# Rotary embedding on one core: tables of 16 rows, batches as runs of 2048 rows, the first tile stored whole

## The chip, the cores and the metric

The kernel runs on one core of a Trainium2 chip. The metric is the device time of one execution in microseconds (us); lower is better. Each time below is from the profile of one execution or from repeated runs without a profile. The engines named are PE (TensorE, matrix products), DVE (VectorE), ACT (ScalarE), POOL (GpSimd) and SP (SyncE). Transfers between DRAM and the on-chip memory (SBUF) are issued by ACT and SP and carried by 16 DMA engines, which take packets from two queues: q10 holds what ACT issues (loads), q1 what SP issues (stores).

## What is computed

A rotary position embedding in fp32 on x of shape (16, 512, 1024): 16 batches, 512 positions, 16 heads of 64. The output has the shape (16, 512, 16, 64).

```python
x = x.reshape(batch, seq, num_heads, head_dim)
x1, x2 = (x[..., :half_dim].copy(), x[..., half_dim:].copy())
cos = cos[None, :, None, :].copy()
sin = sin[None, :, None, :].copy()
rotated = np.concatenate([x1 * cos - x2 * sin, x1 * sin + x2 * cos], axis=-1)
```

33.5 MB are read and 33.5 MB written. cos and sin are 512 x 32 each; a row of x (one position of one batch) uses the table row of its position.

## The kernel before

**Layout.** The 16 x 512 = 8192 rows of x are cut into 8 runs of two batches, 1024 consecutive rows each. Partition p of a run holds 8 consecutive rows (R2), 32 KB, so that one run is one piece of 4 MB, contiguous in DRAM. A run is one tile of 8 rows per partition, except for the first and the last run, which are two tiles of 4 rows (R1) each: tiles 0 and 1, then 2 to 7, then 8 and 9. Below, "row u" is the u-th of the 64 rows per partition, in order; one row is 128 partitions x 1024 elements. Because the 64 partitions of a batch hold 8 positions each, the table on a partition needs 8 rows.

**Tables.** cos and sin are loaded in the natural order, 4 positions to a partition, into `stage` (L173). The table in the layout of x comes from PE: `pick` (L176, made by ACT from an identity matrix) selects every second partition, once from 0 and once from 1, and two products of `pick` with `stage` (L199, L200) put 2 x 4 table rows into `tab_ps`, in PSUM. ACT then copies the sines to SBUF twice, negated (L178) and as they are (L179), as `s_sb`. DVE reads the cosines directly from `tab_ps`. POOL and DVE start with x only when `s_sb` is there (L244, L262). For the row that DVE multiplies by the sine itself (row 3 of a whole tile, V2), one DVE instruction writes the negated sine row beside the plain one (`v_table`, L265).

**Per row.** DVE multiplies x by cos into one of 3 PSUM buffers `t1_ps` (L286). POOL multiplies x, with its halves swapped, by the signed sine into one of 8 buffers `t2_sb` (L252), mostly two rows at a time; for V2 rows DVE does it (L279). The sum is made in one of two ways and overwrites x in `x_sb`: DVE adds both (L297), or, for rows u with u % 8 in 1, 3, 5 (PE2), PE adds `t2` to the PSUM buffer through the identity (L216) and ACT copies the result (L183).

**Order and queues.** Each engine's program is written out by hand, with semaphores between them; nothing is scheduled by a compiler. `x_sb` is a ring of 40 rows, five 4 MB tiles. ACT issues the loads of tiles 0 to 5 at once (L152), with the loads of cos and sin behind tile 0. The other four are issued in ACT's program after row 17, 25 and 33 (LAG): before each, ACT waits until the store of the rows that stood in that place has landed (L186; `sem_out`, `stores_of`), and ACT's copies (L183) of later rows stand behind this wait. SP issues a store for each tile when its last row is added (L160): so the first run leaves as two stores of 2 MB, after row 3 and after row 7. At the end SP waits for all stores that nobody else has waited for (L161).

Of the kernel before, what the change touches and what calls it, by code (L numbers as in the profile page):

```python
# [6 lines left out]
def bass_split_heads_rope_kernel(  # L7
# [16 lines left out]
    batch, seq, dim = x.shape  # L24
    H = int(num_heads)
    HD = dim // H
    HALF = HD // 2
    P = 128
    R1 = seq // P
    R2 = 2 * R1  # L30
    assert R1 * P == seq and R1 == 4 and batch % 2 == 0

    fp32 = mybir.dt.float32
    bf16 = mybir.dt.bfloat16
# [2 lines left out]
    COPY = mybir.ActivationFunctionType.Copy  # L37


    runs = batch // 2  # L40
    tiles = []
    for c in range(runs):
        if c in (0, runs - 1):
            tiles += [(c, 0, R1), (c, R1, R1)]
        else:
            tiles.append((c, 0, R2))
    NT = len(tiles)
    RING = 5 * R2

# [2 lines left out]
    EARLY = (NU - RING) // R2  # L52


    V_ROW = 3
    PE2 = [R1 <= u < NU - R1 and u % R2 in (1, 3, 5) for u in range(NU)]
    V2 = [tiles[t][2] == R2 and r == V_ROW for t, r in rows]

    def count(flags):
        return [sum(flags[: u + 1]) for u in range(NU)]  # L60
# [16 lines left out]
    with ExitStack() as stack:  # L77
        x_sb = stack.enter_context(nc.sbuf_tensor([P, RING, H, 2, HALF], fp32))
        t2_sb = stack.enter_context(nc.sbuf_tensor([P, NT2, H, 2, HALF], fp32))
        stage = stack.enter_context(nc.sbuf_tensor([P, 2, R1 * HALF], fp32))  # L80
        s_sb = stack.enter_context(nc.sbuf_tensor([P, R2, 2, HALF], fp32))
        ident = stack.enter_context(nc.sbuf_tensor([P, P], fp32))
        pick = stack.enter_context(nc.sbuf_tensor([P, 2, 2, P // 2], fp32))
        zero = stack.enter_context(nc.sbuf_tensor([P, BANK], bf16))
        tab_ps = stack.enter_context(nc.psum_tensor([P, 2, 2, R1, HALF], fp32))
        t1_ps = stack.enter_context(nc.psum_tensor([P, NT1, H * HD], fp32))
        sem_in = [stack.enter_context(nc.semaphore(f"in{t}")) for t in range(NT)]
        sem_out = [stack.enter_context(nc.semaphore(f"out{k}")) for k in range(EARLY)]
# [14 lines left out]
        sem_a = stack.enter_context(nc.semaphore("act"))  # L103

        def table_row(u):
            return u % R2

        xr = x.rearrange("(c b) (s r) d -> c (b s) r d", b=2, r=R2)
        outr = out.rearrange("(c b) (s r) h d -> c (b s) r (h d)", b=2, r=R2)
        xs = x_sb[:].rearrange("p n h t d -> p n (h t d)")  # L110

        def in_dram(view, t):
            c, r0, n = tiles[t]
            return view[c][:, r0:r0 + n, :].rearrange("p r d -> p (r d)")

        def in_sbuf(t):
            c, r0, n = tiles[t]
            k = (c * R2 + r0) % RING
            return x_sb[:, k:k + n].rearrange("p n h t d -> p (n h t d)")

        def where(u):
# [3 lines left out]
        def swapped(k):  # L125
            return x_sb[:, k, :, ::-1, :]
# [19 lines left out]

        def stores_of(k):

            return sum(c == k for c, _, _ in tiles)

        def load(eng, t):
            eng.dma_start(in_sbuf(t), in_dram(xr, t)).then_inc(sem_in[t], 16)  # L152
# [1 line left out]
        def on_sync(sp):  # L154
            for u in range(NU):
                t, r, k = where(u)
                if r == tiles[t][2] - 1:
                    wait_added(sp, u)
                    k = u // R2
                    sp.dma_start(in_dram(outr, t), in_sbuf(t)).then_inc(sem_out[k] if k < EARLY else sem_rest, 16)  # L160
            sp.wait_ge(sem_rest, 16 * sum(stores_of(k) for k in range(EARLY, NU // R2)))  # L161

        def on_scalar(ae):
            later = {}
            for t, (c, r0, n) in enumerate(tiles):
                if c * R2 + r0 + n <= RING:
                    load(ae, t)
                else:

                    later.setdefault((c * R2 + r0 - RING) // R2 * R2 + R2 - 1 + LAG, []).append(t)  # L170
                if t == 0:
                    for i, (table, sem) in enumerate(((cos, sem_cos), (sin, sem_sin))):
                        ae.dma_start(stage[:, i, :], table.rearrange("(s r) d -> s (r d)", r=R1)).then_inc(sem, 16)  # L173

            ae.wait_ge(sem_i, 2)
            ae.activation(pick[:], ident[:].rearrange("q (s h) -> q h s", h=2)[:, :, None, :].broadcast_to([P, 2, 2, P // 2]), COPY).then_inc(sem_g, 1)  # L176
            ae.wait_ge(sem_t, 2)
            ae.activation(s_sb[:, :, 0, :].rearrange("p (h r) d -> p h r d", h=2), tab_ps[:, :, 1], COPY, scale=-1.0)  # L178
            ae.activation(s_sb[:, :, 1, :].rearrange("p (h r) d -> p h r d", h=2), tab_ps[:, :, 1], COPY).then_inc(sem_s, 1)  # L179
            for u in range(NU):  # L180
                if PE2[u]:
                    ae.wait_ge(sem_e, n_pe[u])
                    ae.activation(xs[:, u % RING, :], t1_ps[:, u % NT1, :], COPY).then_inc(sem_a, 1)  # L183
                for t in later.get(u, ()):
                    k = tiles[t][0] - RING // R2
                    ae.wait_ge(sem_out[k], 16 * stores_of(k))  # L186
                    load(ae, t)

        def on_tensor(pe):
            pe.wait_ge(sem_z, 1)  # L190
            for k in range(NT1):
                for b in range(EH):
                    pe.matmul(  # L193
                        t1_ps[:, k, b * BANK:(b + 1) * BANK], zero[:, 0:P], zero[:], start=True, stop=True
                    ).then_inc(sem_w, 1)
            pe.wait_ge(sem_g, 1)
            pe.wait_ge(sem_cos, 16)
            pe.wait_ge(sem_sin, 16)
            for h in range(2):  # L199
                pe.matmul(  # L200
                    tab_ps[:, h].rearrange("p c r d -> p (c r d)"),
                    pick[:, h].rearrange("q b s -> q (b s)"),
                    stage[:].rearrange("q c f -> q (c f)"),
                    start=True,
                    stop=True,
                ).then_inc(sem_t, 1)
            for u in range(NU):
                if not PE2[u]:
                    continue
                pe.wait_ge(sem_m, u + 1)  # L210

                if not V2[u]:
                    pe.wait_ge(sem_p, n_pool[u])
                t2 = t2_sb[:, u % NT2, :, :, :].rearrange("p h t d -> p (h t d)")
                for b in range(EH):
                    ins = pe.matmul(  # L216
                        t1_ps[:, u % NT1, b * BANK:(b + 1) * BANK],
                        ident[:],
                        t2[:, b * BANK:(b + 1) * BANK],
                        start=False,  # L220
                        stop=True,
                        skip_group_check=True,
                    )
                ins.then_inc(sem_e, 1)
# [34 lines left out]
        def on_vector(ve):  # L259
            ve.memset(zero[:], 0.0).then_inc(sem_z, 1)  # L260
            ve.wait_ge(sem_w, NT1 * EH)
            ve.wait_ge(sem_s, 1)  # L262

            def v_table():
                ve.tensor_scalar_mul(tab_ps[:, 0, 1, V_ROW - 1, :], tab_ps[:, 0, 1, V_ROW, :], -1.0).then_inc(sem_c, 1)  # L265

            first_v = V2.index(True)

            def mul(u):
                t, r, k = where(u)  # L270
                if r == 0:
                    ve.wait_ge(sem_in[t], 16)
                if (t, r) == (2, 0):
                    v_table()
                if u == first_v:
                    ve.wait_ge(sem_c, 1)
                if V2[u]:
                    wait_t2_free(ve, u)
                    ve.tensor_tensor(t2_sb[:, u % NT2, :, :, :], swapped(k), over_heads(tab_ps[:, 0, 1, V_ROW - 1:V_ROW + 1, :]), mult)  # L279
                if u >= NT1:  # L280
                    v = u - NT1
                    if PE2[v]:
                        ve.wait_ge(sem_a, n_pe[v])
                    else:
                        ve.wait_ge(sem_v, n_comb[v])
                ve.tensor_tensor(  # L286
                    t1_ps[:, u % NT1, :].rearrange("p (h d) -> p h d", d=HALF),
                    x_sb[:, k, :, :, :].rearrange("p h t d -> p (h t) d"),
                    tab_ps[:, table_row(u) // R1, 0, table_row(u) % R1, :][:, None, :].broadcast_to([P, 2 * H, HALF]),
                    mult,  # L290
                ).then_inc(sem_m, 1)

            def comb(u):
                t, r, k = where(u)
                ve.wait_ge(sem_m, u + 1)
                ve.wait_ge(sem_p, n_pool[u])
                ve.tensor_tensor(  # L297
                    xs[:, k, :],
                    t1_ps[:, u % NT1, :],
                    t2_sb[:, u % NT2, :, :, :].rearrange("p h t d -> p (h t d)"),  # L300
                    add,
                ).then_inc(sem_v, 1)

            for u in range(NU + LEAD):
                if u < NU:
                    mul(u)
                if u >= LEAD and not PE2[u - LEAD]:
                    comb(u - LEAD)
# [39 lines left out]
```

## Time and profile before

| what | us |
|---|---|
| median of 3 runs (161.21 to 161.39) | 161.34 |
| the profiled execution | 161.35 |
| its span, first to last instruction | 159.9 |
| busy in the span: POOL, DVE | 131.8, 129.3 |
| busy in the span: PE, ACT | 66.7, 23.7 |
| DVE's and POOL's first instruction on x | 11.68, 11.67 |
| stores issued: first run, two halves | 22.30, 33.67 |
| stores issued: next three 4 MB tiles | 49.99, 65.83, 82.88 |
| last store issued | 150.83 |

The span is what the profile shows of the execution; 1.45 us of the execution's time lie outside it. DMA moved 67.25 MB in the span, a mean of 420 GB/s. Landing times of transfers, which the prediction uses, are the times of the semaphore updates that the DMA engines make; packet times are from the trace's records of DMA packets.

In the profile's lines, "x4" is a count, "[7.23 <-DMA ...]" is the engine's idle time just before and what ended it, and 128x256 is partitions x elements.

### The profile page before, as it was taken

The numbers are of one execution on the slowest core, as the hardware profiler recorded it, in microseconds if no ns is written. First come the engines' busy times: TensorE is split into PE (matmuls) and PEld (weight loads), VectorE is DVE, ScalarE is ACT, GpSimd is POOL, SyncE is SP. The second block draws the span as 40 slices with busy tenths as digits, with TensorE's granted clock in tenths as the row PEclk, the third lists the DMA queues.
The fourth block names the chain that finished last, engine by engine and source line by source line (L and its number), as shares of the span: only waits on it lengthen the run. The fifth ranks groups of instructions, "written<-read, shape, count | busy, mean of one in ns | idle before, by whom it ended". The sixth has DMA issues, their size and how long they took to land.

```text
span 159.9 us, 494 instructions
## 1 busy us (share of the span) xinstructions
PE 66.7 (42%) x94; PEld 22.6 (14%) x94; DVE 129.3 (81%) x115; ACT 23.7 (15%) x25; POOL 131.8 (82%) x41
## 2 busy tenths in 40 slices
PE   6050006338932762286209540098509860880000
PEld 1020002012301220122002110022102220220000
DVE  0009986799999999999799927999999989989700
ACT  0410000202220222020400204002500250031000
POOL 1009999999999999999999999599999999598000
PEclk9999999999995799569965998555985589567555
DMA  5999998999999999999999999999999999999896
GB/s 164 411 441 459 393 508 344 447 406 426 471 406 447 479 393 395 492 418 402 418 492 393 418 492 402 402 475 389 479 397 418 451 418 488 410 402 484 373 438 279
DMA packets 3169, 67.25 MB, mean 420 GB/s; under 512 B 352, under 2 KB 608, under 8 KB 608
## 3 DMA queue, kind: packets, MB, share of 16 engines
q10 hardware_dynamic: 1728, 33.69, 49.8%
q1 hardware_dynamic: 1440, 33.56, 48.7%
q14 instruction: 1, 0.01, 0.0%
HBM read 33.69 MB, written 33.55 MB: 420 GB/s over the span
## 4 chain that ended last, share of the span: by engine, by line
DMA 49%; DVE 16%; POOL 13%; issue 7%; PE 6%; ACT 2%; ACTq 1%; DVEq 0%; SPq 0%
DMA x_sb<-in_x_dram 27%; DMA out_dram<-x_sb 18%; POOL t_sb L252 13%; DVE x_sb L297 8%; DVE t_ps L286 6%; PE t_ps L216 5%; DMA stage<-in_sin_dram 4%; DVE t_sb L279 2%; ACT x_sb L183 1%; PE tab_ps L200 1%; ACTq L152 0%; ACTq L173 0%; ACT s_sb L178 0%; ACT s_sb L179 0%; DVE tab_ps L265 0%
## 5 line engine op out<-in xcount | busy, mean ns | idle before, releaser
L252 POOL TENSOR_TENSOR t_sb<-x_sb,s_sb 128x2048 f32<-128x2048 f32 (+1 forms) x35 | 131.1, 3775 | 14.9 <-ACT s_sb L179 10.3
L216 PE MATMUL t_ps<-t_sb,ident 128*128 128x512 f32 x84 | 61.9, 888 | 70.6 <-DVE t_ps L286 48.8
L286 DVE TENSOR_TENSOR t_ps<-x_sb,tab_ps 128x1024 f32<-128x1024 f32 x64 | 76.7, 1221 | 17.4 <-ACT s_sb L179 10.5
L297 DVE TENSOR_TENSOR x_sb<-t_ps,t_sb 128x1024 f32<-128x1024 f32 x43 | 52.3, 1219 | 3.2 <-POOL t_sb L252 3.1
L183 ACT ACTIVATE x_sb<-t_ps 128x1024 f32<-128x1024 f32 x21 | 21.3, 1024 | 111.6 <-PE t_ps L216 100.2
L216 PEld LDWEIGHTS t_ps<-t_sb,ident 128*128 128x128 f32 x84 | 20.7, 273 | 111.4 <-DVE t_ps L286 78.8
L279 DVE TENSOR_TENSOR t_sb<-x_sb,tab_ps 128x1024 f32<-128x1024 f32 x6 | 7.3, 1215 | 0.0
L200 PE MATMUL tab_ps<-stage,pick 128*128 128x256 f32 x4 | 2.0, 667 | 4.8 <-DMA stage<-in_sin_dram 4.8
L193 PE MATMUL t_ps<-zero 128*128 128x512 bf16 x6 | 2.7, 630 | 1.3 <-DVE zero L260 1.3
L200 PEld LDWEIGHTS tab_ps<-stage,pick 128*128 128x128 f32 x4 | 1.2, 324 | 5.9 <-issue 5.7
L176 ACT ACT_TABLE_LOAD x1 | 1.3, 1283 | 4.8 <-issue 4.8
L193 PEld LDWEIGHTS t_ps<-zero 128*128 128x128 bf16 x6 | 0.7, 138 | 2.3 <-DVE zero L260 1.2
L178 ACT ACTIVATE s_sb<-tab_ps 128x256 f32<-128x256 f32 x1 | 0.4, 384 | 4.4 <-PE tab_ps L200 4.4
L260 DVE MEMSET zero<- 128x256 uint32 x1 | 0.3, 272 | 0.9 <-PEq L330 0.9
L227 POOL MEMSET ident<- 128x128 f32 x1 | 0.2, 205 | 0.3 <-POOLq L330 0.3
L176 ACT ACTIVATE pick<-ident 128x256 f32<-128x256 f32 x1 | 0.4, 430 | 0.0
L179 ACT ACTIVATE s_sb<-tab_ps 128x256 f32<-128x256 f32 x1 | 0.4, 378 | 0.0
L229 POOL TENSOR_SCALAR_AFFINE_SELECT ident<-ident 128x128 f32<-128x128 f32 x1 | 0.3, 294 | 0.1
L330 POOL MEMSET const-float32-0.0<- 128x1 f32 x1 | 0.1, 99 | 0.3 <-issue 0.3
L265 DVE TENSOR_SCALAR tab_ps<-tab_ps 128x32 f32<-128x32 f32 x1 | 0.2, 189 | 0.0
L330 POOL MEMSET const-bfloat16-1.0<- 128x1 bf16 x1 | 0.1, 102 | 0.0
L330 POOL MEMSET const-uint8-127<- 128x1 uint8 x1 | 0.1, 102 | 0.0
(1 smaller groups left out, 0.1 us busy)
## 6 DMA issues: line engine op xcount, KB each, us to landing
x_sb<-in_x_dram ACTq DMA_DIRECT2D x6, 4096.0 KB, 33.5
out_dram<-x_sb SPq DMA_DIRECT2D x6, 4096.0 KB, 25.0
x_sb<-in_x_dram ACTq DMA_DIRECT2D x4, 2048.0 KB, 19.9
out_dram<-x_sb SPq DMA_DIRECT2D x4, 2048.0 KB, 14.9
stage<-in_cos_dram ACTq DMA_DIRECT2D x1, 64.0 KB, 7.3
stage<-in_sin_dram ACTq DMA_DIRECT2D x1, 64.0 KB, 7.0
```

Of the source, the lines that this page charges most:

```text
L176: ae.activation(pick[:], ident[:].rearrange("q (s h) -> q h s", h=2)[:, :, None, :].broadcast_to([P, 2, 2, P // 2]), COPY).then_inc(sem_g, 1)
L178: ae.activation(s_sb[:, :, 0, :].rearrange("p (h r) d -> p h r d", h=2), tab_ps[:, :, 1], COPY, scale=-1.0)
L179: ae.activation(s_sb[:, :, 1, :].rearrange("p (h r) d -> p h r d", h=2), tab_ps[:, :, 1], COPY).then_inc(sem_s, 1)
L183: ae.activation(xs[:, u % RING, :], t1_ps[:, u % NT1, :], COPY).then_inc(sem_a, 1)
L193: pe.matmul(t1_ps[:, k, b * BANK:(b + 1) * BANK], zero[:, 0:P], zero[:], start=True, stop=True).then_inc(sem_w, 1)
L200: pe.matmul(tab_ps[:, h].rearrange("p c r d -> p (c r d)"), pick[:, h].rearrange("q b s -> q (b s)"), stage[:].rearrange("q c f -> q (c f) ...
L216: ins = pe.matmul(t1_ps[:, u % NT1, b * BANK:(b + 1) * BANK], ident[:], t2[:, b * BANK:(b + 1) * BANK], start=False, stop=True, skip_group ...
L252: pl.tensor_tensor(t2_sb[:, u % NT2:u % NT2 + n], x_sb[:, k:k + n, :, ::-1, :], table[:, :, None, :, :].broadcast_to([P, n, H, 2, HALF]), ...
L279: ve.tensor_tensor(t2_sb[:, u % NT2, :, :, :], swapped(k), over_heads(tab_ps[:, 0, 1, V_ROW - 1:V_ROW + 1, :]), mult)
L286: ve.tensor_tensor(t1_ps[:, u % NT1, :].rearrange("p (h d) -> p h d", d=HALF), x_sb[:, k, :, :, :].rearrange("p h t d -> p (h t) d"), tab_ ...
L297: ve.tensor_tensor(xs[:, k, :], t1_ps[:, u % NT1, :], t2_sb[:, u % NT2, :, :, :].rearrange("p h t d -> p (h t d)"), add,).then_inc(sem_v, 1)
L330: nc = _bacc.Bacc("TRN2", target_bir_lowering=False, num_devices=1)
```

## The change

- A run is now four batches, 2048 rows, 16 rows (R4) per partition; there are four runs of 8 MB. Tiles stay at 8 rows: a run has two, rows 0 to 7 and rows 8 to 15 of each partition. A whole tile is thus 128 pieces of 32 KB that stand 64 KB apart in DRAM. The very first and the very last tile are still split in two of 4 rows, so the list has the same 10 tiles of the same sizes in the same order, and the ring and the order of the rows on every engine are as before.
- 32 partitions hold a batch, 16 positions each, so the table has 16 rows: `pick` selects every fourth partition, four times (128 x 512 elements, before 128 x 256), PE makes four products instead of two, ACT waits for all of them, and ACT's two copies of the sines are twice as large. `tab_ps` takes twice the PSUM.
- The V2 rows are now table row 3 or 11, so `v_table` has two instructions.
- The two halves of the first tile are still loaded separately, but stored by one transfer of 4 MB after row 7. The load that follows it in the ring waits for that one.

```diff
+    R4 = 4 * R1
-    runs = batch // 2
+    runs = batch // 4
     tiles = []
     for c in range(runs):
-        if c in (0, runs - 1):
-            tiles += [(c, 0, R1), (c, R1, R1)]
-        else:
-            tiles.append((c, 0, R2))
+        for r0 in range(0, R4, R2):
+            if (c, r0) in ((0, 0), (runs - 1, R4 - R2)):
+                tiles += [(c, r0, R1), (c, r0 + R1, R1)]
+            else:
+                tiles.append((c, r0, R2))
...
-    V_ROW = 3
+    V_ROWS = (3, 11)
...
-        s_sb = stack.enter_context(nc.sbuf_tensor([P, R2, 2, HALF], fp32))
+        s_sb = stack.enter_context(nc.sbuf_tensor([P, R4, 2, HALF], fp32))
...
-        pick = stack.enter_context(nc.sbuf_tensor([P, 2, 2, P // 2], fp32))
+        pick = stack.enter_context(nc.sbuf_tensor([P, 4, 4, P // 4], fp32))
...
-        tab_ps = stack.enter_context(nc.psum_tensor([P, 2, 2, R1, HALF], fp32))
+        tab_ps = stack.enter_context(nc.psum_tensor([P, 4, 2, R1, HALF], fp32))
...
-        xr = x.rearrange("(c b) (s r) d -> c (b s) r d", b=2, r=R2)
-        outr = out.rearrange("(c b) (s r) h d -> c (b s) r (h d)", b=2, r=R2)
+        xr = x.rearrange("(c b) (s r) d -> c (b s) r d", b=4, r=R4)
+        outr = out.rearrange("(c b) (s r) h d -> c (b s) r (h d)", b=4, r=R4)
...
-            return sum(c == k for c, _, _ in tiles)
+            return 1 if k == 0 else sum((c * R4 + r0) // R2 == k for c, r0, _ in tiles)
...
-                if r == tiles[t][2] - 1:
+                if r == tiles[t][2] - 1 and u >= R2 - 1:
                     wait_added(sp, u)
                     k = u // R2
-                    sp.dma_start(in_dram(outr, t), in_sbuf(t)).then_inc(sem_out[k] if k < EARLY else sem_rest, 16)
+                    src, dst = in_sbuf(t), in_dram(outr, t)
+                    if k == 0:
+                        src = x_sb[:, 0:R2].rearrange("p n h t d -> p (n h t d)")
+                        dst = outr[0][:, 0:R2, :].rearrange("p r d -> p (r d)")
+                    sp.dma_start(dst, src).then_inc(sem_out[k] if k < EARLY else sem_rest, 16)
...
-            ae.activation(pick[:], ident[:].rearrange("q (s h) -> q h s", h=2)[:, :, None, :].broadcast_to([P, 2, 2, P // 2]), COPY).then_inc(sem_g, 1)
-            ae.wait_ge(sem_t, 2)
+            ae.activation(pick[:], ident[:].rearrange("q (s j) -> q j s", j=4)[:, :, None, :].broadcast_to([P, 4, 4, P // 4]), COPY).then_inc(sem_g, 1)
+            ae.wait_ge(sem_t, 1)
...
-            for h in range(2):
-                pe.matmul(
-                    tab_ps[:, h].rearrange("p c r d -> p (c r d)"),
-                    pick[:, h].rearrange("q b s -> q (b s)"),
+            for j in range(4):
+                ins = pe.matmul(
+                    tab_ps[:, j].rearrange("p c r d -> p (c r d)"),
+                    pick[:, j].rearrange("q b s -> q (b s)"),
                     stage[:].rearrange("q c f -> q (c f)"),
                     start=True,
                     stop=True,
-                ).then_inc(sem_t, 1)
+                )
+            ins.then_inc(sem_t, 1)
...
             def v_table():
-                ve.tensor_scalar_mul(tab_ps[:, 0, 1, V_ROW - 1, :], tab_ps[:, 0, 1, V_ROW, :], -1.0).then_inc(sem_c, 1)
+                for r in V_ROWS:
+                    ve.tensor_scalar_mul(tab_ps[:, r // R1, 1, r % R1 - 1, :], tab_ps[:, r // R1, 1, r % R1, :], -1.0).then_inc(sem_c, 1)
...
-                    ve.wait_ge(sem_c, 1)
+                    ve.wait_ge(sem_c, 2)
```

More of the change, by code (lines that the diff above doesn't have):

```diff
@@ L30, in bass_split_heads_rope_kernel @@
     R2 = 2 * R1
-    assert R1 * P == seq and R1 == 4 and batch % 2 == 0
+    R4 = 4 * R1
+    assert R1 * P == seq and R1 == 4 and batch % 4 == 0
     fp32 = mybir.dt.float32
@@ L52, in bass_split_heads_rope_kernel @@
     EARLY = (NU - RING) // R2
-    V_ROW = 3
+    V_ROWS = (3, 11)
     PE2 = [R1 <= u < NU - R1 and u % R2 in (1, 3, 5) for u in range(NU)]
-    V2 = [tiles[t][2] == R2 and r == V_ROW for t, r in rows]
+    V2 = [tiles[t][2] == R2 and r == V_ROWS[0] for t, r in rows]
     def count(flags):
@@ L105, in table_row @@
         def table_row(u):
-            return u % R2
-        xr = x.rearrange("(c b) (s r) d -> c (b s) r d", b=2, r=R2)
-        outr = out.rearrange("(c b) (s r) h d -> c (b s) r (h d)", b=2, r=R2)
+            return u % R4
+        xr = x.rearrange("(c b) (s r) d -> c (b s) r d", b=4, r=R4)
+        outr = out.rearrange("(c b) (s r) h d -> c (b s) r (h d)", b=4, r=R4)
         xs = x_sb[:].rearrange("p n h t d -> p n (h t d)")
@@ L117, in in_sbuf @@
             c, r0, n = tiles[t]
-            k = (c * R2 + r0) % RING
+            k = (c * R4 + r0) % RING
             return x_sb[:, k:k + n].rearrange("p n h t d -> p (n h t d)")
@@ L165, in on_scalar @@
             for t, (c, r0, n) in enumerate(tiles):
-                if c * R2 + r0 + n <= RING:
+                if c * R4 + r0 + n <= RING:
                     load(ae, t)
                 else:
-                    later.setdefault((c * R2 + r0 - RING) // R2 * R2 + R2 - 1 + LAG, []).append(t)
+                    later.setdefault((c * R4 + r0 - RING) // R2 * R2 + R2 - 1 + LAG, []).append(t)
                 if t == 0:
@@ L175, in on_scalar @@
             ae.wait_ge(sem_i, 2)
-            ae.activation(pick[:], ident[:].rearrange("q (s h) -> q h s", h=2)[:, :, None, :].broadcast_to([P, 2, 2, P // 2]), COPY).then_inc(sem_g, 1)
-            ae.wait_ge(sem_t, 2)
-            ae.activation(s_sb[:, :, 0, :].rearrange("p (h r) d -> p h r d", h=2), tab_ps[:, :, 1], COPY, scale=-1.0)
-            ae.activation(s_sb[:, :, 1, :].rearrange("p (h r) d -> p h r d", h=2), tab_ps[:, :, 1], COPY).then_inc(sem_s, 1)
+            ae.activation(pick[:], ident[:].rearrange("q (s j) -> q j s", j=4)[:, :, None, :].broadcast_to([P, 4, 4, P // 4]), COPY).then_inc(sem_g, 1)
+            ae.wait_ge(sem_t, 1)
+            ae.activation(s_sb[:, :, 0, :].rearrange("p (j r) d -> p j r d", j=4), tab_ps[:, :, 1], COPY, scale=-1.0)
+            ae.activation(s_sb[:, :, 1, :].rearrange("p (j r) d -> p j r d", j=4), tab_ps[:, :, 1], COPY).then_inc(sem_s, 1)
             for u in range(NU):
@@ L184, in on_scalar @@
                 for t in later.get(u, ()):
-                    k = tiles[t][0] - RING // R2
+                    k = (tiles[t][0] * R4 + tiles[t][1] - RING) // R2
                     ae.wait_ge(sem_out[k], 16 * stores_of(k))
@@ L275, in mul @@
                 if u == first_v:
-                    ve.wait_ge(sem_c, 1)
+                    ve.wait_ge(sem_c, 2)
                 if V2[u]:
                     wait_t2_free(ve, u)
-                    ve.tensor_tensor(t2_sb[:, u % NT2, :, :, :], swapped(k), over_heads(tab_ps[:, 0, 1, V_ROW - 1:V_ROW + 1, :]), mult)
+                    ve.tensor_tensor(t2_sb[:, u % NT2, :, :, :], swapped(k), over_heads(tab_ps[:, table_row(u) // R1, 1, table_row(u) % R1 - 1:table_row(u) % R1 + 1, :]), mult)
                 if u >= NT1:
```

## The prediction

> **What bounds the kernel now.** I read the page's slices and DMA queues first, then stretches of the span, the chain that ended last, the timeline around its stalls and the last store.
>
> ```profile
> DMA  5999998999999999999999999999999999999896
> ...
> q10 hardware_dynamic: 1728, 33.69, 49.8%
> q1 hardware_dynamic: 1440, 33.56, 48.7%
> ```
>
> The 16 DMA engines have hardly a free slice; the load queue (q10) and the store queue (q1) together fill 98.5% of the span. In the table of stretches (stretch, length, five engines' busy time, granted clock, DMA share, GB/s):
>
> ```profile
> 24.00:36.00 12.00, 4.99 (x6) 1.89 (x7) 9.50 (x10) 1.02 (x1) 12.00 (x4) 1.00 0.96 396
> ...
> 98.00:138.00 40.00, 20.14 (x26) 7.13 (x27) 39.25 (x36) 6.15 (x7) 35.59 (x9) 0.68 1.00 433
> ```
>
> 433 GB/s is the ceiling; only 24 to 36 us lies clearly under it. The 67.25 MB don't change. By the trace's packet records a DMA engine is busy 157.6 us on average, the first packet starts at 1.81, the last engine stops at 159.57 (the mean one at 158.9), and the last semaphore is in at 159.91. So the time can fall only by slow packets (those over their usual length cost 1.33 us per engine: 0.81 before 5 us, 0.46 in loads from 24.9 to 41, little else) and by the 0.7 us between mean and slowest engine; it rises as soon as the engines run dry. The question is how near the compute comes to letting them. The chain, in order of time:
>
> ```profile
> 65.83 29.31 DMA out_dram<-x_sb
> 95.14 0.02 issue
> 95.16 0.33 ACTq L152
> ```
>
> ACT waits in order for the third 8-row tile's store (issued 65.83, landed 95.14) before it may load the last tiles (L186), and its copies stand behind:
>
> ```profile
> 96.06 1.94 ACT L183 ACTIVATE x_sb<-t_ps 128x1024 f32<-128x1024 f32 x2 [7.23 <-DMA out_dram<-x_sb]
> 97.12 2.36 DVE L286 TENSOR_TENSOR t_ps<-x_sb,tab_ps 128x1024 f32<-128x1024 f32 x2 [4.14 <-ACT x_sb L183]
> ```
>
> DVE stands idle for 4.14 us until then; from 98 to 138 it is busy 39.25 of 40 us. So the last store's issue hangs on that landing: 150.83 = 95.14 + 55.7. How much room it has (instructions of L160, last stretch):
>
> ```profile
> L160 SPq DMA_DIRECT2D out_dram<-x_sb x1: 332/332/332, 150.8 to 150.8; - x1
> ...
> DMA to landing us min/median/max: 9.1/9.1/9.1
> ```
>
> Alone it would need 1.0 us to its first packet (the first load: issue 0.80, packet 1.81, on idle engines), 2.097 MB / 433 GB/s = 4.84, and 0.34 from the last packet to the semaphore: 6.2. It takes 9.1, so **2.9 us of slack** lie in the backlog ahead of it. The 4 MB store before the last two has 14.6 - (1.0 + 9.69 + 0.34) = 3.6.
>
> **The change, part by part.**
>
> *Table.* Now:
>
> ```profile
> 8.85 2.04 PE L200 MATMUL tab_ps<-stage,pick 128*128 128x256 f32 x4 [4.85 <-DMA stage<-in_sin_dram]
> 10.93 0.38 ACT L178 ACTIVATE s_sb<-tab_ps 128x256 f32<-128x256 f32 x1 [4.41 <-PE tab_ps L200]
> 11.21 0.38 ACT L179 ACTIVATE s_sb<-tab_ps 128x256 f32<-128x256 f32 x1
> 11.67 2.35 POOL L252 TENSOR_TENSOR t_sb<-x_sb,s_sb 128x1024 f32<-128x1024 f32 x1 [10.30 <-ACT s_sb L179]
> ```
>
> Two selections make four records, 0.43 us from start to start (9.40, 9.83, 10.26). Four make eight: 4 x 0.43 = +1.72. The two ACT copies go from 256 to 512 elements. ACT takes 384 ns for 256 and 1024 ns for 1024 (L183), thus 0.83 ns an element: +0.21 each, +0.42. Sum **+2.14** until POOL and DVE start (bounds: 1.7, if the copies cost nothing more, and 2.7, twice of 2.04 + 0.66). The copy into pick doubles too (0.43, at most 0.86), but ends by 7.0 and PE waits for the sine until 8.85: nothing. Behind ACT's later wait stand only its own copies; all six early loads are issued by 4.6. The second table row on DVE (L265, 189 ns, 0.10 to the next start) adds 0.1. None of this starves the DMA: until tile 5 lands at 70.3 the load queue is full.
>
> *The first tile's store.* SP drops the issue at 22.30; one of 4 MB goes out when the second did, plus the delay: 33.67 + 2.14 + 0.1 = 35.9. Nothing else stands in SP's queue. Between 22 and 36 us loads take the whole rate instead, so the engines stay full. The first store now gets its first packets 4.0 to 5.5 us after issue (26.3 to 27.8), queued behind load packets; I take the same, 39.9 to 41.4. Then the queues alternate packet by packet (a 4 MB store beside loads lands every 19.3 us, twice 9.7): 8 packets on each engine and 7 loads between, 15 x 1.214 = 18.2, and 0.4 to land: 58.5 to 60.0. The slowest engine decides, so 59.4, against 56.3 now (33.67 + 22.6): **+3.1**. The next two stores follow at 19.3 and 19.55 us as now, since they are waiting by then; the release at 95.14 becomes 98.3, and the last store's issue 150.83 becomes 153.9. The 4.14 us of DVE idle time hide the compute's own 2.2, not this delay. It exceeds the slack of 2.9 by 0.2. Bounds: if the first packet came 1.0 us after issue, 55.5 to 56, no delay, 0; if 60.0 and 2.7 for the table, +4.3, a loss of 1.4. The 3.6 of the store before stay enough for 3.1.
> Half packets take 611 ns and whole ones 1214: eight pairs an engine become whole, -0.06.
>
> *Load order.* Loads get ahead by what stores fall behind, so the last half tile, which POOL awaits 1.94 us at 138.16, lands some 3 us sooner. No gain: DVE has 11.5 of 12 us busy from 138 to 150.
>
> *Addresses.* Every piece stays 16 or 32 KB; only its pitch in DRAM doubles to 64 KB. Before shows half tiles: 16 KB at 32 KB pitch, 26.8 bytes/ns, against 27.0 for whole, contiguous tiles. That row is near, so I take 0. The other bound: if what slowed the load of 24.9 to 36.9 us (55 packets, 0.46 us per engine) struck each of eight tiles, 8 x 0.46 = +3.7; if it went away, -0.5.
> The Trainium skill, DMA: Bandwidth & Descriptors, Latency and other measured facts, has a rule against wide power-of-two pitches: rows 512 KiB apart ran at 207 GB/s per direction where the full rate was 214. By that, an estimate of 3.3% of 157.6, +5.2 us; it measures a pitch eight times this one, and no run here shows it.
>
> **Sum.** 159.9 + 0.2 - 0.06 = 160.05; the profiled execution's 161.35 has 1.45 outside its span, so 161.5. Its 161.35 is the median's 161.34.
>
> **The rivals.**
> A. Forecast: DMA hides nearly everything, 161.5; own range 161.1 to 161.7.
> B. The tail starves (slower). One mechanism: the first store's landing, passed on through ACT's waits to the last store. It decides when that landing comes over 2.9 us later than 56.3; each us beyond costs a us. At 60.0 and 2.7 it is 162.8; the middle is 162.2. For it: slack and shift are nearly equal. Against: the granted clock, which stretches PE in the tail (0.68 now), may give some back.
> C. The pitch slows packets: 161.35 + 3.7 = 165; from about 1 us on it shows, and it would sit in all stretches. Against it, the half tiles. The Trainium skill's rule above is this case.
> D. Faster. The slow packets of 24.9 to 41 come with the first half store, and fewer, later stores avoid them (0.46), and the engines end closer together (up to 0.7): 160.2 to 161.0, the middle 160.7. Against: they begin at 24.9, before the store's first packet at 26.3, so they may belong to that load.
> E. That the change doesn't do what it says: runs of 2048 rows lengthen no piece, so nothing is gained from them; this is inside A.
>
> **How the numbers follow.** A 0.42, B 0.27, C 0.09, D 0.22. 0.2% is 0.32 us, about what measurement can tell: within it lies A (161.0 to 161.7), 0.42; slower B and C, 0.36; faster D, 0.22. 160.7 to 163.0 holds A, B and the upper part of D; below it some 0.07 remain, above it C and little of B, 0.1.
>
> **What would show it.** Right: POOL's first multiply at 13.8, the first store issued at 35.9 and landing near 59.4, ACT's long wait ending near 98.3, the last store issued near 153.9 and landing in about 6.2 to 6.5, DMA's slices full to the end. Wrong: a landing near 56 (no shift, the loss is 0), long packets in other stretches than 24 to 36 (C), a 24 to 36 stretch at 433 GB/s (D), or the last store out before 153 with an end later than 160.2.

## The result, and the profile after

Over 19 runs of each, taken in turn, the changed kernel's median is 162.59 us and the old one's 161.44: a ratio of 1.0072, 95% interval 1.0054 to 1.0090. It is slower by 0.7%. Its runs also spread more: 161.42 to 163.63, before 161.14 to 161.92. The profiled execution took 162.75 us, its span is 161.3.

The page's slices and queue table of the changed kernel:

```profile
DMA  6999999999999999999999999999999999899797
...
q10 hardware_dynamic: 1728, 33.69, 49.6%
q1 hardware_dynamic: 1296, 33.56, 48.4%
```

The bytes are the same; the store queue has 144 packets fewer (the eight pairs of half packets on each engine, and the semaphore writes of one transfer). New are the slices under 9 near the end. The stretches of the changed kernel (columns as before):

```profile
24.00:36.00 12.00, 3.51 (x4) 1.17 (x4) 8.91 (x11) 1.02 (x1) 12.00 (x3) 0.92 1.01 434
36.00:44.00 8.00, 5.77 (x8) 1.85 (x8) 8.00 (x8) 1.58 (x2) 8.00 (x4) 0.69 0.95 356
98.00:138.00 40.00, 17.93 (x26) 5.78 (x24) 35.86 (x32) 8.08 (x8) 35.93 (x10) 0.74 1.00 433
138.00:150.00 12.00, 6.63 (x8) 2.37 (x8) 11.52 (x11) 2.05 (x2) 11.49 (x4) 0.72 0.92 396
```

From 98 to 138 us the ceiling is as before. 36 to 44 us, where the first store now begins, runs at 356 GB/s (449 before), and from 138 to 150, where only stores are left, the engines idle for a part: 396 GB/s. The same stretch before:

```profile
138.00:150.00 12.00, 5.41 (x7) 1.53 (x6) 11.52 (x11) 2.05 (x2) 9.15 (x3) 0.64 0.99 429
```

The start, in the timeline:

```profile
8.76 3.75 PE L206 MATMUL tab_ps<-stage,pick 128*128 128x256 f32 x8 [4.77 <-DMA stage<-in_sin_dram]
12.55 0.60 ACT L184 ACTIVATE s_sb<-tab_ps 128x512 f32<-128x512 f32 x1 [5.35 <-PE tab_ps L206]
13.04 0.59 ACT L185 ACTIVATE s_sb<-tab_ps 128x512 f32<-128x512 f32 x1
13.72 2.34 POOL L259 TENSOR_TENSOR t_sb<-x_sb,s_sb 128x1024 f32<-128x1024 f32 x1 [12.35 <-ACT s_sb L185]
```

POOL starts at 13.72 instead of 11.67, 2.05 us later. The chain and the timeline around ACT's long wait:

```profile
68.08 31.64 DMA out_dram<-x_sb
99.75 0.33 ACTq L154
```

```profile
100.67 1.94 ACT L189 ACTIVATE x_sb<-t_ps 128x1024 f32<-128x1024 f32 x2 [7.19 <-DMA out_dram<-x_sb]
101.73 2.36 DVE L294 TENSOR_TENSOR t_ps<-x_sb,tab_ps 128x1024 f32<-128x1024 f32 x2 [3.96 <-ACT x_sb L189]
```

The same wait as before, ending 4.6 us later (99.75, before 95.16). And the stores (L166) of three stretches: the first one, the 4 MB store before the last two, and the last two:

```profile
L166 SPq DMA_DIRECT2D out_dram<-x_sb x1: 377/377/377, 35.8 to 35.8; - x1
...
DMA to landing us min/median/max: 25.0/25.0/25.0
```

```profile
L166 SPq DMA_DIRECT2D out_dram<-x_sb x1: 332/332/332, 139.7 to 139.7; - x1
...
DMA to landing us min/median/max: 11.2/11.2/11.2
```

```profile
L166 SPq DMA_DIRECT2D out_dram<-x_sb x2: 332/332/333, 148.6 to 155.0; - x2
...
DMA to landing us min/median/max: 6.3/6.7/7.2
```

The last store leaves at 155.0 and takes 6.3 us, what it needs alone (6.2 by the prediction's sum); before it took 9.1. So nothing stood in the queue ahead of it: the engines had run dry. The 4 MB store before takes 11.2, also about what it needs alone (11.0; 14.6 before). In the packet records an engine idles 0.8 us on average before that 4 MB store and 0.6 before the last one, and all 16 engines stop within 0.13 us of each other (160.77 to 160.90), because they all wait for the same issue. Before, they stopped between 158.56 and 159.57, each when its own queue was empty. The two gaps add up to 1.4, as much as the span's growth (161.3 - 159.9), but the sum has more terms. The mean engine stops 1.9 us later (158.9 before, 160.8 now): 1.4 for the gaps and some 0.5 for load packets that became longer. The last engine, which decides, stops only 1.3 us later, because before it stopped 0.7 after the mean one and now it stops with the others.

### The profile page after: what moved, and what is told of

Read it like the earlier page. It is cut to its first block, busy times and chain, and to the rows that moved or that the text cites. A ratio compares the mean times of both kernels' runs of the same rounds, so it can differ in the third digit from the quotient of the medians.

```text
span 161.3 us, 502 instructions
## 1 busy us (share of the span) xinstructions
PE 68.6 (43%) x98; PEld 24.3 (15%) x98; DVE 129.3 (80%) x116; ACT 24.7 (15%) x25; POOL 131.7 (82%) x41
## 4 chain that ended last, share of the span: by engine, by line
POOL 27%; DMA 24%; DVE 21%; PE 10%; issue 9%; ACT 3%; ACTq 1%; DVEq 0%; SPq 0%
POOL t_sb L259 27%; DMA out_dram<-x_sb 20%; DVE x_sb L305 10%; DVE t_ps L294 10%; PE t_ps L223 7%; DMA stage<-in_sin_dram 4%; ACT x_sb L189 3%; PE tab_ps L206 2%; DVE t_sb L287 1%; ACTq L154 1%; ACT s_sb L184 0%; ACT s_sb L185 0%; ACTq L179 0%; DVE tab_ps L273 0%; DVEq L304 0%
## 5 line engine op out<-in xcount | busy, mean ns | idle before, releaser
L206 PE MATMUL tab_ps<-stage,pick 128*128 128x256 f32 x8 | 3.8, 651 | 4.8 <-DMA stage<-in_sin_dram 4.8
L206 PEld LDWEIGHTS tab_ps<-stage,pick 128*128 128x128 f32 x8 | 2.5, 330 | 6.2 <-issue 5.6
L184 ACT ACTIVATE s_sb<-tab_ps 128x512 f32<-128x512 f32 x1 | 0.6, 597 | 5.3 <-PE tab_ps L206 5.3
L182 ACT ACTIVATE pick<-ident 128x512 f32<-128x512 f32 x1 | 1.1, 1107 | 0.0
L185 ACT ACTIVATE s_sb<-tab_ps 128x512 f32<-128x512 f32 x1 | 0.6, 592 | 0.0
```

The costliest lines, as they stand in the source:

```text
L182: ae.activation(pick[:], ident[:].rearrange("q (s j) -> q j s", j=4)[:, :, None, :].broadcast_to([P, 4, 4, P // 4]), COPY).then_inc(sem_g, 1)
L184: ae.activation(s_sb[:, :, 0, :].rearrange("p (j r) d -> p j r d", j=4), tab_ps[:, :, 1], COPY, scale=-1.0)
L185: ae.activation(s_sb[:, :, 1, :].rearrange("p (j r) d -> p j r d", j=4), tab_ps[:, :, 1], COPY).then_inc(sem_s, 1)
L206: ins = pe.matmul(tab_ps[:, j].rearrange("p c r d -> p (c r d)"), pick[:, j].rearrange("q b s -> q (b s)"), stage[:].rearrange("q c f -> q ...
```

## The experiments

Three theories stood at the start. The chain theory: the first tile's store lands late, ACT's waits hand that on, the last store comes after the queue is empty. The pitch theory: pieces 64 KB apart in DRAM are slower. The start theory: the table's 2 us by themselves reach the end. Each experiment ran beside the kernel before, whose median was 161.29 to 161.43 us in these series. The ratios are to the kernel before of the same series; they are not quotients of the two medians and differ from these by up to 0.15%.

**1. The changed kernel with two half stores again.**

```diff
-            return 1 if k == 0 else sum((c * R4 + r0) // R2 == k for c, r0, _ in tiles)
+            return sum((c * R4 + r0) // R2 == k for c, r0, _ in tiles)
...
-                if r == tiles[t][2] - 1 and u >= R2 - 1:
+                if r == tiles[t][2] - 1:
...
-                    if k == 0:
-                        src = x_sb[:, 0:R2].rearrange("p n h t d -> p (n h t d)")
-                        dst = outr[0][:, 0:R2, :].rearrange("p r d -> p (r d)")
```

> The changed kernel (2048-row runs, 16-row table), but the first tile leaves as two half stores again. Chain theory (the first tile's store lands late, ACT's wait passes it on, the last store comes too late to keep the DMA engines fed): the halves go out near 24.3 and 35.8 us, the second lands near 58 instead of 60.8, the last store is issued near 152.5 instead of 155.0, within the slack that ends near 153.8: 161.3 to 161.7 us. Pitch theory (pieces 64 KB apart are slower): stays near 162.6. Start theory (the table 2 us later costs 1:1 at the end): stays near 162.6 or above.

161.49 us, ratio 1.0012 (0.9999 to 1.0026). ACT's long wait ends at 96.80, and the last store (source view of its line):

```profile
L163 SPq DMA_DIRECT2D out_dram<-x_sb x1: 332/332/332, 152.1 to 152.1; - x1
...
DMA to landing us min/median/max: 8.2/8.2/8.2
```

152.1 is inside the slack. Pitch and table are both still there, and the loss is gone but for 0.12%, which the interval does not tell from none: neither makes the loss by itself.

**2. The kernel before, only the store made whole.** The same edit of stores as in the change, with `tiles` and `xr` as before.

```diff
-                if r == tiles[t][2] - 1:
+                if r == tiles[t][2] - 1 and u >= R2 - 1:
...
+                    if k == 0:
+                        src = x_sb[:, 0:R2].rearrange("p n h t d -> p (n h t d)")
+                        dst = outr[0][:, 0:R2, :].rearrange("p r d -> p (r d)")
```

> The kernel before (1024-row runs, 8-row table), with only the first tile's store made whole. Chain theory: issue 33.7, landing 25 us later as in the changed kernel, 58.7; last store near 153: 161.4 to 161.9 us. Pitch theory and start theory: 161.4, no change, since neither pitch nor table changes.

161.42 us, ratio 1.0013 (1.0005 to 1.0022). The store is issued at 33.58 and lands at 57.64, 1.1 us sooner than expected; the last is issued at 151.58 and takes 8.3 us. Also inside the slack.

**3. The kernel before, only the slower table.**

```diff
-            for h in range(2):
-                pe.matmul(
-                    tab_ps[:, h].rearrange("p c r d -> p (c r d)"),
-                    pick[:, h].rearrange("q b s -> q (b s)"),
+            for j in range(4):
+                ins = pe.matmul(
+                    tab_ps[:, j].rearrange("p c r d -> p (c r d)"),
+                    pick[:, j % 2].rearrange("q b s -> q (b s)"),
...
-            ae.activation(s_sb[:, :, 0, :].rearrange("p (h r) d -> p h r d", h=2), tab_ps[:, :, 1], COPY, scale=-1.0)
+            ae.activation(s_sb[:, :, 0, :].rearrange("p (j r) d -> p j r d", j=4), tab_ps[:, :, 1], COPY, scale=-1.0)
```

> The kernel before with only the slower table (four products, ACT copies of 512 elements; the second half repeats the first and is not read); runs of 1024 rows, first tile in two half stores. Chain theory: POOL starts near 13.7 instead of 11.7, the second half store lands near 57.7 instead of 56.3, the last store is issued near 152.2, inside the slack: 161.3 to 161.6 us, although all compute starts 2 us later. Start theory (the later start passes to the end by itself): 163.

161.56 us, ratio 1.0013 (1.0001 to 1.0025). The second half store lands at 58.96, 1.3 us later than expected, the last store is issued at 152.47 and takes 7.4 us. All compute started 2 us later and the end hardly moved: the start theory falls.

**4. The kernel before with both, runs of 1024 rows.** The edits of 2 and 3 together; every piece in DRAM as before.

> The kernel before with the whole first store and a table that takes as long as the new one (four products, ACT copies of 512 elements; its second half repeats the first and is not read), but with 1024-row runs, pieces contiguous. Chain theory: as the changed kernel, first store near 35.8, landing near 60.8, last store near 155, 162.3 to 162.9 us. Pitch theory: 161.4, as before. Start theory: 162.3 to 162.9.

162.59 us, ratio 1.0095 (1.0074 to 1.0115). The last two stores:

```profile
L164 SPq DMA_DIRECT2D out_dram<-x_sb x2: 332/332/333, 147.7 to 155.3; - x2
...
DMA to landing us min/median/max: 6.3/7.4/8.5
```

The changed kernel's whole loss, with contiguous runs: the pitch theory falls. It also shows that the two parts don't add up: each alone costs 0.13%, both 0.95%. Each alone stays within the slack, both together leave it.

**5. The kernel before, whole store, held by a wait.** Table, start and addresses as before; SP waits with the first store until row 8 is added, not row 7.

```diff
-                    wait_added(sp, u)
+                    wait_added(sp, 8 if u == R2 - 1 else u)
```

> The kernel before with the whole first store, held until row 8 is added instead of row 7; table and addresses as before, compute starts at 11.7. Issue near 35.8, as in the changed kernel. Chain theory: landing near 60.5, last store near 155, 162.3 to 162.8 us. Start theory and pitch theory: 161.4.

162.52 us, ratio 1.0070 (1.0056 to 1.0084). Issue 35.91, landing 60.27, last store 155.12, taking 6.3 us. Holding the first store by 2.3 us, with nothing else changed against experiment 2, gives the whole loss. That is the chain theory's cause by itself.

**6. The same, held until row 10.**

```diff
-                    wait_added(sp, u)
+                    wait_added(sp, 10 if u == R2 - 1 else u)
```

> The same, held until row 10 is added: issue near 40.4, 4.6 us later than with row 8. Chain theory, one us of time for each us beyond the slack: landing near 65, last store near 159.5 to 160, 166 to 168 us. If something else caps the loss (compute with its own spare time), 162.5 to 164.

163.44 us (162.27 to 164.35), ratio 1.0127 (1.0084 to 1.0169). A miss: 4.4 us more delay don't cost 4 us more. ACT's program in the timelines, first held until row 8, then until row 10; each line is the end of ACT's wait for the next store's landing:

```profile
60.30 0.34 ACTq L152 DMA_DIRECT2D x_sb<-in_x_dram  x1
...
80.08 0.34 ACTq L152 DMA_DIRECT2D x_sb<-in_x_dram  x1
...
99.43 0.89 ACTq L152 DMA_DIRECT2D x_sb<-in_x_dram  x2
```

```profile
62.93 0.34 ACTq L152 DMA_DIRECT2D x_sb<-in_x_dram  x1
...
79.87 0.34 ACTq L152 DMA_DIRECT2D x_sb<-in_x_dram  x1
...
99.25 0.88 ACTq L152 DMA_DIRECT2D x_sb<-in_x_dram  x2
```

The first landing is 2.6 us later, the second and third are not. In the queue table of 59.6 to 66.8 us of the second kernel q1 has 96.5% of the packets' time, where the first shows both queues:

```profile
q1 hardware_dynamic: 107, 2.98, 96.5%
```

The six loads that ACT may issue ahead have landed, the next one still waits for the first store, and the stores have the engines to themselves until they have caught up. So the delay has a cap, and the last store leaves at 154.89 as in experiment 5. The profiled execution (162.64) fits that; three of six runs, at 164.2 to 164.4, had no profile, and why they are longer stays open.

**7. The changed kernel with LAG 14.** ACT copies rows 33, 35 and 37 before it waits for the landing.

```diff
-    LAG = 10
+    LAG = 14
```

> The changed kernel with LAG 14 instead of 10: ACT waits for the store's landing after the copies of rows 33, 35 and 37, not before the last two of them, so its copies no longer stand behind it. Chain theory: ACT's waits of 13.9 us for stores and DVE's 4.0 us idle at 98 go, the last store is issued 2 to 4 us sooner (151 to 153), the DMA engines stay fed: 161.2 to 161.7 us. Pitch theory: stays near 162.6. Start theory: little change, 162.3 or more.

161.72 us over ten runs, one of which took 164.13; the ratio of the other nine is 1.0032 (1.0015 to 1.0048). The first store is as late as in the changed kernel (landing 60.49), ACT's waits for stores are gone from the list of waits, and the last store leaves 6.6 us sooner, more than the 2 to 4 expected:

```profile
L166 SPq DMA_DIRECT2D out_dram<-x_sb x1: 333/333/333, 148.4 to 148.4; - x1
...
DMA to landing us min/median/max: 11.8/11.8/11.8
```

A backlog stands ahead of it again: 11.8 us to land against 6.2 alone. So it is ACT's wait in front of its copies that carries the delay from the first store to the last. It makes over half of the loss: some 0.3% is left.

**8. The kernel before with LAG 14.** The same edit.

> The kernel before with LAG 14 instead of 10, so ACT's copies do not stand behind the store waits. Chain theory: DVE's 4.1 us idle goes, the last store is issued some 4 us sooner, but the DMA engines were full already: 161.2 to 161.5 us, no change. If the compute still set the end of the kernel before: 158 to 160.

161.27 us, ratio 0.9996 (0.9987 to 1.0005). DVE's idle time before ACT's copies falls from 6.9 to 0.8 us in total, but the last store moves only from 150.8 to 149.8, not by 4: POOL and DVE now wait for the last half tile's load (POOL 4.34 us before 138.23). And the time doesn't move: the old kernel's end is the DMA engines', not the compute's.

**9 and 10. What is left with LAG 14.** First the changed kernel with half stores and LAG 14 (the edits of 1 and 7), then runs of 1024 rows with whole store, slow table and LAG 14 (the edits of 4 and 7).

> The changed kernel with the first tile in two half stores and LAG 14: the 64 KB pitch and the slow table stay, the late store and ACT's waits in front of copies are gone. Theory that what is left of the loss with LAG 14 alone (0.3%) comes from load packets slowed where a late whole store begins: 161.3 to 161.5 us, slow packets near 0.6 us per engine. Pitch theory for that rest: 161.7.

> 1024-row runs (contiguous pieces), whole first store, slow table, LAG 14. Burst theory for the rest of 0.3%: 161.6 to 161.9 us, slow load packets of 0.8 to 1.0 us per engine near 37 to 40 us. Pitch theory for the rest: 161.3 to 161.4.

161.60 us, ratio 1.0013 (1.0000 to 1.0026), and 161.93, ratio 1.0024 (1.0009 to 1.0039). The second one keeps its loss with contiguous pieces, which the pitch theory for the rest did not expect. The first one's 161.60 lies between the two forecasts and decides nothing. The slow load packets cost 0.61 us per engine in the first and 1.04 in the second, but of the 1.04 only 0.54 lie near the first store (38 to 41 us), where the theory had put 0.8 to 1.0; the other 0.50 lie at 75 to 77 us. So the rest of 0.2 to 0.3% goes with the slow packets in all, not with those at the first store alone. The intervals overlap, and its cause stays open.

**11. The changed kernel once more.** No edit.

> The changed kernel once more, for a second profile, since its runs spread from 161.4 to 163.6 us. Chain theory: the last store's issue moves with the time of the run, one us for one us, 155.0 us in the first profile at 162.75; where it differs, PE's granted clock after the release near 99 us should differ (rows that PE adds take 2.0 or 3.8 us).

162.89 us; last store issued at 155.15, landing 6.3 us later, against 155.00 in the run of 162.75. The two runs are too near each other to test what makes others take 161.4 or 163.6. Over the 19 runs time and PE's mean granted clock go against each other (correlation -0.46), which fits an end that hangs on rows summed by PE, but it was not tried.

## Why the prediction was right or wrong

The direction that it gave the most weight to, no change, did not come; its case B did, by the mechanism and at the place that it named, and 162.59 lies between that case's middle (162.2) and its upper price (162.8). The time lies in the stated range of 160.7 to 163.0 because that range held case B; the point forecast, 161.5, was 1.1 us too low.

- **The bound.** Right. With all of ACT's waits taken off the compute (experiment 8), the old kernel keeps its time.
- **The table.** +2.14 forecast, +2.05 measured; 0.597 us for an ACT copy of 512 elements, as worked out from the two known sizes. The copy into `pick` took 1.11 us, over the bound of 0.86, and still ended before PE needed it.
- **The first store.** Issue 35.9 forecast, 35.79 measured. **The landing is the term that was mis-sized:** 59.4 forecast, 60.80 measured, a shift of 4.5 us and not 3.1. What it had wrong is the wait for the first packet. Over the 16 engines the store's first packets start at 40.08 to 42.34, 4.3 to 6.6 us after the issue, where the prediction took 4.0 to 5.5 (39.9 to 41.4) over from the old kernel. The load packets ahead of them were longer than usual: 26 of those that start at 37.0 to 40.4 us took 1.4 to 2.7 us instead of 1.21, 0.99 us per engine in all (the records don't name the engine; packets are matched by their times). The rest of the term was right: the engines' landings spread from 58.55 to 60.80, 18.5 us behind their first packets, where the prediction's 15 x 1.214 and 0.4 make 18.6. The latest engine counts. Experiments 2, 4 and 5 have the same 18.5 us (last first packets at 39.14, 42.03 and 41.77, landings at 57.64, 60.49 and 60.27).
- **The hand-on.** Right: the release moved from 95.16 to 99.75 and the last store from 150.83 to 155.00, 55.3 us behind the release where the prediction carried 55.7.
- **The slack.** Right for the last store: 155.00 - 150.83 - 2.9 = 1.3 of loss, 1.4 measured. Wrong for the 4 MB store before it: "the 3.6 of the store before stay enough for 3.1" falls with the 3.1. That store's issue moved by 4.2 us, and the first and larger of the two gaps (0.8) lies before it.
- **Load order.** Right: the last half tile landed at 134.2 instead of 138.1, and it gained nothing.
- **Addresses.** Right to take 0: experiments 1 and 4. The Trainium skill's rule against wide power-of-two pitches (DMA: Bandwidth & Descriptors, Latency and other measured facts) speaks of rows 512 KiB apart and more. At 64 KB none of it is seen: 162.59 us with contiguous runs and slow table (ratio 1.0095) against 162.59 in the changed kernel (1.0072). Case C falls. Its sign, long packets outside 24 to 36 us, did come, but contiguous runs have them too: 0.80 us per engine at 38 to 41 us in experiment 4.
- **Case D.** Half right: the slow packets come with the first store and not with the load of 24.9 us. What fails is that a later, whole store avoids them. Its sign came, 24 to 36 us did run at 434 GB/s, but the slow packets moved with the first store to 37 to 40 us and cost 0.99 us instead of 0.46.

Shown by the experiments: the late first store is enough (5), neither of its two causes is enough alone (2, 3), the loss comes without the pitch (4), and ACT's in-order wait carries over half of it (7). No variant beat the old kernel; 161.27 is the nearest, and equal to it.

## What to carry to other kernels

Where DMA is the bound, ask how long before it runs dry each transfer is issued: a transfer that takes 9.1 us where it would need 6.2 alone has 2.9 us of slack, and two delays that are harmless alone (1.4 and 2.7 us at the first run's last landing, experiments 2 and 3) can together exceed it. Follow a late transfer through the in-order waits on its landing to the last one that is issued; a wait that is put behind the copies which others need (LAG 14 for 10) cuts that path. A loss can have a cap where the other queue runs empty and frees the engines (experiment 6).

## What the runs showed of the hardware that was not expected

In every kernel, load packets become longer soon after the first store is issued, though their number of bytes is the same: the first long ones start 1.1 to 2.6 us after the issue, for stores issued anywhere from 22.2 to 40.3 us. Near that store their time over the usual 1.21 us is 0.46 to 0.69 us per engine where it is issued by 33.6 us, and 0.56 to 1.07 where it is issued at 35.6 to 40.3; single packets of 32 KB reach 2.9 us. Later stores have no such stretch in most kernels, but experiments 6 and 10 have a second one from 75 to 79 us, of 0.59 and 0.53 us per engine. What slows the packets was not tried.
